# One hybrid decoder layer on one core: 1/rms per token through DRAM, fewer small products, one FFN unit moved

## The chip, the cores and the metric

The kernel runs on one core of a Trainium2 chip. Its engines work at the same time, each through its own queue in order: TensorE (PE in the profile, with its weight loads as PEld), VectorE (DVE), ScalarE (ACT), GpSimd (POOL) and SyncE (SP), which here only issues transfers. POOL issues transfers too. The metric is the device time of one execution in microseconds. The kernel before was run three times: 818.30, 817.38 and 817.83 us, a median of 817.83 us.

## The reference

A decoder layer for 512 tokens of width 1024, in float32. The parts that the change touches:

```python
def rms_norm(x, g):
    xf = x.astype(jnp.float32)
    y = xf * lax.rsqrt(jnp.mean(xf * xf, axis=-1, keepdims=True) + EPS)
    return (y * g.astype(jnp.float32)).astype(x.dtype)

def stick_breaking_attention(q, k, v):
    for i in range(nb):                      # 4 blocks of 128 queries
        z = jnp.einsum('bqhd,bkhd->bhqk', q[:, i * BLOCK:L], k[:, :L]) * (d ** -0.5)
        causal = jnp.arange(L)[None, :] < t
        log_1m = jnp.where(causal, jax.nn.log_sigmoid(-z), 0.0)
        between = lax.cumsum(log_1m, axis=3, reverse=True) - log_1m
        a = jnp.where(causal, jnp.exp(jax.nn.log_sigmoid(z) + between), 0.0)
        outs.append(jnp.einsum('bhqk,bkhd->bqhd', a, v[:, :L]))

def reference(...):
    u = rms_norm(h, ln_mix_pre[l])
    proj = jnp.einsum('bsd,de->bse', u, w_in[l])       # queries, keys, values, gates of three branches
    mkv = jnp.einsum('bmd,de->bme', rms_norm(mem, ln_mem[l]), w_mem_kv[l])
    ...                                                # three attentions, gated, merged, w_out, residual
    a = jax.nn.silu(u @ w_gate[l]) * (u @ w_up[l])     # second norm ahead of it
    ffn = a @ w_down[l]
    h = h + rms_norm(ffn, ln_ffn_post[l])
```

## The kernel before, in words

Each matrix operand is held as two float32r parts, hi and lo: ScalarE rounds to hi (line 134), VectorE subtracts to get lo (line 135), and a product is three matmuls, hi by hi, hi by lo and lo by hi (mm3, lines 166 to 168). Single matmuls go through mm (line 171). On PE the three of an mm3 follow each other; when a weight unit's hi or lo isn't there, PE waits.

Weights come through a Stream. A unit is one block of weights: a load on SP's queue, a split into hi and lo, and the matmuls. Loads run up to four or five units ahead of the matmuls and splits three, in the order in which the units were added. The attention code asks the stream for so many microseconds of matmuls between its own steps, so that PE has work while the other engines do softmax and masks. A planner then orders each engine's instructions: program order is the priority, an instruction is drawn forward when its engine is free and its inputs are there in the planner's estimated times, and code inside tc.high_priority() comes first. Lines 503 to 545 stand in a block whose own order is fixed; other instructions may come between.

Norms. The projections take x times its gain without 1/rms, and the result is scaled as it leaves PSUM. So 1/rms per token is needed in two layouts. rb is a [128 x n] tile with the tokens along the free dimension, the same row in every partition; rs is a [128 x n/128] tile with one token per partition and column. rstd_of (line 218) makes both from the sums of squares per partition: a product with a matrix of ones gives rb's sums in every partition (tile ss_x or ss_m); products of 128 tokens as stationary operand with a single column of ones give rs's (tile st_x for x, a corner of ss_m for mem). Each goes through rsqrt (line 209), two ScalarE and four VectorE instructions. For x, n is 512 and the sums lie in one 512-wide tile. For mem, n is 256 and the tile holds two halves, which the products add in PSUM. rb_x is used by each projection's evacuation (line 288), rs_x by that of the values (L333), rb_m by the memory's keys (line 380), rs_m by its values (line 398).

Values. val (line 322) accumulates 320 columns for four blocks of tokens in four PSUM banks out of a pool of six, first for h = 0, then for h = 1. The banks of the first come free when VectorE has scaled them into v_all (line 333).

Stick-breaking. sb_head (line 605) makes for each of eight heads the scores z of four key blocks in three PSUM tiles, the last two blocks in the same tile, and adds a large negative number on the diagonal blocks by a bf16 product of the identity with the mask, one for each key block (lines 626 and 627).

On POOL lie the casts of constants, the clears of the tiles qbl and kal (line 268), the adds of mem's squares (line 368), the transfers that build the bias (bscr and bias, lines 584 and 593), and later the accumulating loads of the FFN.

FFN. Gate and up are computed for eleven pairs of 128-wide column tiles by a seven-product scheme (p1, p5, p6, p3, p7, p2, p4 for each pair n), each product a unit of 24 matmuls of 256 columns. Its weight operands are sums of weight blocks, made by a plain load on SP (g_raw) and accumulating loads on POOL (g_plus) in a pool of nine buffers, and for p6 and p3 of the later pairs by an add on VectorE as well (g_sum, line 986). The list seq (lines 1230 to 1233) sets the order of the units; the loads are tied to positions in it: for p5 of pair n the plain load four units ahead and the accumulating load two units ahead, and the same for p7. The token operands are called B11, B21, T1, N2, N22, T3 and T4; p3 uses N22, p5 uses T1, p4 uses T4.

Of the kernel before, what the change touches and what calls it, by code (L numbers as in the profile page):

```python
# [10 lines left out]
F32 = mybir.dt.float32  # L11
# [3 lines left out]
ALU = mybir.AluOpType  # L15
AX = mybir.AxisListType

P = 128
D = 1024
S = 512  # L20
# [83 lines left out]
def tile_kernel(ctx, tc, a):  # L104
    nc = tc.nc
# [6 lines left out]
    drm = ctx.enter_context(tc.tile_pool(name="drm", bufs=1, space=bass.MemoryType.DRAM))  # L112
# [3 lines left out]
    cst = first.enter_context(tc.tile_pool(name="cst", bufs=1))  # L116

    def ck(name, dt=F32):
        return ckp.tile([P, 512], dt, tag="ck", name=name)

    def small(name, n=4):
        return sm.tile([P, 8], F32, tag="s", name=name)[:, :n]
# [4 lines left out]
    def aps(name):  # L127
        return psa.tile([P, 512], F32, tag="a", name=name)

    st = {}  # L130
# [33 lines left out]
    def mm3(out, l, r, start, stop):  # L164
        (lh, ll), (rh, rl) = l, r
        nc.tensor.matmul(out, lh, rh, start=start, stop=False, skip_group_check=True)  # L166
        nc.tensor.matmul(out, lh, rl, start=False, stop=False, skip_group_check=True)  # L167
        nc.tensor.matmul(out, ll, rh, start=False, stop=stop, skip_group_check=True)  # L168

    def mm(out, l, r, start, stop):  # L170
        nc.tensor.matmul(out, l, r, start=start, stop=stop, skip_group_check=True)  # L171

    def cols(hl, o, n):
        return hl[0][:, o : o + n], hl[1][:, o : o + n]
# [7 lines left out]
    def fn(*args, **kw):  # L182

        ins = nc.scalar.activation(*args, **kw)  # L184
        for p in pin:
            after(ins, p)
        since.append(ins)
        return ins
# [10 lines left out]
    def const(name, shape, pool=cst):  # L199
        t = pool.tile(shape, F32, name=f"c_{name}")  # L200
        nc.sync.dma_start(t[:, :], a[name])
        return t
# [3 lines left out]
    ones = cst.tile([P, P], F32, name="ones")  # L206
    nc.vector.memset(ones[:, :], 1.0)

    def rsqrt(r, v, t, ss):

        fn(t, ss, AF.Ln, bias=eps_t, scale=1.0 / D)
        nc.vector.tensor_scalar(v, ss, 1.0 / D, EPS, op0=ALU.mult, op1=ALU.add)
        fn(r, t, AF.Exp, scale=-0.5)
        nc.vector.scalar_tensor_tensor(t, r, -0.5, r, op0=ALU.mult, op1=ALU.mult)
        nc.vector.tensor_tensor(t, t, v, op=ALU.mult)
        nc.vector.scalar_tensor_tensor(r, t, 1.5, r, op0=ALU.add, op1=ALU.mult)

    def rstd_of(name, acc, n, bank):


        w = acc.shape[1] // n
        ps = bank(f"ss_{name}")
        for i in range(w):
            mm(ps[:, :n], ones[:, :], acc[:, i * n : (i + 1) * n], i == 0, i == w - 1)
        pt = bank(f"st_{name}")[:, : n // P] if n == S else ps[:, n : n + n // P]
        for t in range(n // P):
            for i in range(w):
                mm(pt[:, t : t + 1], acc[:, i * n + t * P : i * n + (t + 1) * P], ones[:, :1], i == 0, i == w - 1)
        rb = cst.tile([P, n], F32, name=f"rb_{name}")
        v, t = ck(f"v_{name}"), ck(f"t_{name}")  # L230
        rsqrt(rb[:, :], v[:, :n], t[:, :n], ps[:, :n])
        rs = cst.tile([P, n // P], F32, name=f"rs_{name}")
        rsqrt(rs[:, :], small(f"v_{name}", n // P), small(f"t_{name}", n // P), pt)
        return rs, rb

    def gained(x, g, h, l):
# [85 lines left out]
    def val(h, q):  # L322
        def gen(hi, lo):
            if q == 0:
                st["pv"] = [aps(f"pv{h}{t}") for t in range(NT)]
            for i in range(3 if q < 2 else 2):
                k = 3 * q + i
                for t in range(NT):
                    x = (u[k][0][:, t * P : (t + 1) * P], u[k][1][:, t * P : (t + 1) * P])
                    mm3(st["pv"][t][:, :320], x, cols((hi, lo), i * 320, 320), k == 0, k == KC - 1)  # L330
                    yield 0.41
                    if k == KC - 1:
                        nc.vector.tensor_scalar(  # L333
                            v_all[:, t * 640 + h * 320 : t * 640 + (h + 1) * 320],
                            st["pv"][t][:, :320],
                            st["rs"][:, t : t + 1],
                            None,
                            op0=ALU.mult,
                        )

        return gen

    v_all = cst.tile([P, NT * 640], F32, name="v_all")
# [90 lines left out]
    for h in range(2):  # L434
        for q in range(3):
            n = 3 if q < 2 else 2
# [111 lines left out]
    ident = const("ident", [P, P], base)  # L548
    ntri = const("ntri", [P, P])
    nmf = const("negm", [P, P])  # L550
    sinks = cst.tile([P, 8], F32, name="sinks")
    nc.sync.dma_start(sinks[:, :], a["sinks"].to_broadcast([P, 8]))
    identb = cst.tile([P, P], BF16, name="identb")
    nc.gpsimd.tensor_copy(identb[:, :], ident[:, :])
    negm = cst.tile([P, P], BF16, name="negmb")
    nc.gpsimd.tensor_copy(negm[:, :], nmf[:, :])
    ntri_r = cst.tile([P, P], F32R, name="ntri_r")
    nc.gpsimd.tensor_copy(ntri_r[:, :], ntri[:, :])
    none = cst.tile([P, P], F32, name="none")
# [38 lines left out]
    SEG = [(0, 0, 512), (1, 0, 384), (2, 0, 256), (2, 256, 128)]  # L598
# [6 lines left out]
    def sb_head(h):  # L605
        c = h // 2
        ks, qs, ql = (st[(x, c, h % 2)] for x in ("kbs", "qbs", "qbl"))
        z = [aps(f"z{h}{i}") for i in range(3)]

        def seg(ts, j):  # L610
            i, o, n = SEG[j]
            return ts[i][:, o : o + n]

        for j in range(4):
            i, o, n = SEG[j]
            kj = slice(j * P, (j + 1) * P)
            if j < 3:
                out, qh, qlo = z[i][:, o : o + n], qs[:, j * P :], ql[:, j * P :]
            else:

                out = z[i][:, o : o + 2 * n]
                qh = qs[:, j * P :].unsqueeze(1).to_broadcast([P, 2, P])
                qlo = ql[:, j * P :].unsqueeze(1).to_broadcast([P, 2, P])
            mm(out, ks[:, kj], qh, j < 3, False)
            mm(out, ks[:, kj], qlo, False, False)
        for i, o, n in SEG:
            mm(z[i][:, o : o + P], identb[:, :], negm[:, :], False, False)
        e = [ck(f"e{h}{i}") for i in range(3)]
        sh = [ck(f"sh{h}{i}", F32R) for i in range(3)]
        sl = [ck(f"sl{h}{i}", F32R) for i in range(3)]  # L630
        for i in range(3):
            x, n = e[i][:, : W[i]], W[i]
            nc.scalar.activation(x, z[i][:, :n], AF.Abs)
            fn(x, x, AF.Exp, scale=-1.0)
            st["chain"] = fn(x, x, AF.Ln, bias=1.0)
            nc.vector.scalar_tensor_tensor(x, z[i][:, :n], 0.0, x, op0=ALU.max, op1=ALU.add)
            if i == 2:

                nc.vector.tensor_tensor(e[i][:, 384:], e[i][:, 128:256], e[i][:, 256:384], op=ALU.add)
                x, n = e[i][:, :], 512  # L640
            nc.vector.tensor_copy(sh[i][:, :n], x)
            nc.vector.tensor_tensor(sl[i][:, :n], x, sh[i][:, :n].bitcast(F32), op=ALU.subtract)
        yield 7.0

        def both(t):

            return t[2][:, :].rearrange("p (b n) -> p b n", b=4)[:, 0:4:3, :]

        for j in range(3):
            for t in (sh, sl):  # L650
                mm(seg(z, j), ntri_r[:, :], seg(t, j), False, j == 2 and t is sl)
        for t in (sh, sl):
            mm(z[0][:, 128:], none_r[:, :], seg(t, 1), False, False)
        for t in (sh, sl):
# [12 lines left out]
        for j in range(4):  # L667
            for i, x in enumerate((st["even"], e)):
                mm(ys[64 * i : 64 * i + 64, j * P :], vcols(j, 128 + (2 * c + i) * 64), seg(x, j), j == 0, j == 3)
        pair_out(SB, c, ys)  # L670
# [412 lines left out]
    rb = {}  # L1083
    bank = {}
# [143 lines left out]

    fs = Stream(None, f_split, LOAD_AHEAD + 1)
    seq = [("p1", 0), ("p2", 0), ("p1", 1), ("p1", 2), ("p2", 1)]  # L1230
    seq += [("p5", 0), ("p6", 0), ("p3", 0), ("p5", 1), ("p7", 0), ("p6", 1), ("p3", 1), ("p4", 0)]
    for n in range(1, HF):
        seq += [(p, n) for p in PROD if (p, n) not in seq]
    at = {x: i for i, x in enumerate(seq)}
# [166 lines left out]
```

## Time and profile before

| What | Value |
|---|---|
| Median of three runs | 817.83 us |
| Profiled execution, its own time | 818.05 us |
| Its span | 816.3 us |
| PE busy | 806.5 us, 99% |
| VectorE busy | 590.2 us, 72% |
| ScalarE busy | 440.2 us, 54% |
| GpSimd busy | 82.7 us, 10% |
| Granted TensorE clock, mean | 0.999 |
| DMA | 112.93 MB, mean 138 GB/s |

The rows of the timeline read: start in us, duration in us (of the whole run of them, where several are merged), engine, line and operation, tile written and tiles read, form, count, and in brackets how long the engine had been idle and what ended that. A row of waits gives the engine, tile and line that waited, what it waited for, the total in us, how often, and the longest. A window's row gives the length and then, for PE, PEld, DVE, ACT and POOL, the busy time with the number of instructions, then the granted clock, the DMA share and GB/s. A row of a tile or a group gives least, median and greatest duration in ns and the first and last start. A row of DMA issues gives the queue, the count, the size and the median us from issue to landing.

### The profile page before, as it was taken

To read this page: it belongs to the slowest core of one execution; us is meant where nothing else is said; L and a number is where in the kernel's file an instruction comes from. 1 tells how busy PE (TensorE), PEld (TensorE's weight loads), DVE (VectorE), ACT (ScalarE), POOL (GpSimd) and SP (SyncE) were. 2 spreads that over 40 slices of the span, in tenths; PEclk is the share of its full clock that TensorE was granted. 3 is DMA by queue.
4 is the path that set the end of the run, shared out by engine and by line. 5 is a ranking of instruction groups with operands and counts; after the bars stand their busy time and mean duration, and the time that the engine had idled before them with its cause. 6 is when DMAs were issued, how large, how long until landed. Compare 5 with 4: busy or idle time off the path is not lost.

```text
span 816.3 us, 12397 instructions
## 1 busy us (share of the span) xinstructions
PE 806.5 (99%) x4753; PEld 706.6 (87%) x4753; DVE 590.2 (72%) x945; ACT 440.2 (54%) x791; POOL 82.7 (10%) x100
## 2 busy tenths in 40 slices
PE   9999999999999999999999999999999999999996
PEld 6899888778788888888888899999999999988885
DVE  7796768556488853774385869977776767798797
ACT  7453757556555542553362666644444455666573
POOL 3002200000000000231003200010000000205200
PEclk9999999999999999999999999999999999999999
DMA  7434524321221223212359945977777763759902
GB/s 267 141 114 128 190 87 128 85 73 52 78 78 53 78 78 102 79 53 78 103 155 352 254 93 142 247 199 201 183 189 178 185 178 94 169 131 223 213 1 103
DMA packets 37563, 112.93 MB, mean 138 GB/s; under 512 B 4352, under 2 KB 6064, under 8 KB 37504
## 3 DMA queue, kind: packets, MB, share of 16 engines
q1 hardware_dynamic: 29184, 86.32, 33.5%
q0 software_dynamic: 7888, 25.43, 16.4%
q8 instruction: 37, 0.61, 0.3%
q10 hardware_dynamic: 432, 0.39, 0.1%
q14 instruction: 22, 0.18, 0.1%
HBM read 108.46 MB, written 3.67 MB: 137 GB/s over the span
## 4 chain that ended last, share of the span: by engine, by line
PE 94%; DVE 3%; ACT 1%; DMA 1%; issue 0%; ACTq 0%; SPq 0%; DVEq 0%
PE g L166 5%; PE g L167 5%; PE g L168 5%; PE gx L166 5%; PE gx L168 5%; PE gx L167 5%; PE z L171 4%; PE br L166 3%; PE br L167 3%; PE br L168 3%; PE gy L168 3%; PE gy L166 3%; PE gy L167 3%; PE x L167 2%; PE x L166 2%; PE x L168 2%
## 5 line engine op out<-in xcount | busy, mean ns | idle before, releaser
L134 ACT CAST hi<-raw 128x1024 fp32r<-128x1024 f32 (+2 forms) x64 | 65.8, 1034 | 110.1 <-issue 50.2
L134 ACT CAST hi<-gw 128x1024 fp32r<-128x1024 f32 x77 | 79.8, 1048 | 82.2 <-DVE gw L986 40.0
L135 DVE TENSOR_TENSOR lo<-gw,hi 128x1024 fp32r<-128x1024 f32 x77 | 93.5, 1223 | 33.6 <-ACT hi L134 33.6
L135 DVE TENSOR_TENSOR lo<-raw,hi 128x1024 fp32r<-128x1024 f32 (+2 forms) x64 | 78.1, 1220 | 17.6 <-ACT hi L134 17.3
L166 PE MATMUL g<-uh,hi 128*128 128x512 f32 x192 | 75.6, 394 | 0.0
L168 PE MATMUL g<-uh,lo 128*128 128x512 f32 x192 | 74.8, 389 | 0.0
L167 PE MATMUL g<-ul,hi 128*128 128x512 f32 x192 | 74.8, 389 | 0.0
L288 DVE SCALAR_TENSOR_TENSOR g<-g,rb_x 128x512 f32<-128x512 f32 x24 | 16.4, 690 | 55.4 <-PE g L168 55.3
L168 PEld LDWEIGHTS g<-uh,lo 128*128 128x128 f32 x192 | 36.0, 188 | 7.6
L166 PEld LDWEIGHTS g<-uh,hi 128*128 128x128 f32 x192 | 36.1, 188 | 7.5 <-issue 0.3
L968 POOL DMA_DIRECT2D gw<-in_w_gu x27 | 23.4, 905 | 188.8 <-DMA gw<-in_w_gu 81.4
L167 PEld LDWEIGHTS g<-ul,hi 128*128 128x128 f32 x192 | 36.1, 188 | 7.1
L134 ACT CAST hi<-r 128x1024 fp32r<-128x1024 f32 (+1 forms) x24 | 23.6, 982 | 19.9 <-PE y L168 5.3
L167 PE MATMUL x<-lo,lh 128*128 128x512 f32 x88 | 34.2, 389 | 0.0
L166 PE MATMUL x<-hi,lh 128*128 128x512 f32 x88 | 34.2, 389 | 0.0
L168 PE MATMUL x<-hi,ll 128*128 128x512 f32 x88 | 34.1, 389 | 0.0
L135 DVE TENSOR_TENSOR lo<-r,hi 128x1024 fp32r<-128x1024 f32 (+1 forms) x24 | 27.1, 1131 | 3.7 <-ACT hi L134 3.6
L184 ACT ACTIVATE e<-e 128x384 f32<-128x384 f32 (+1 forms) x48 | 26.9, 561 | 1.5
L134 ACT CAST hi<-bp 128x512 fp32r<-128x512 f32 x33 | 19.1, 619 | 13.4 <-PE y L168 4.8
L135 DVE TENSOR_TENSOR lo<-bp,hi 128x512 fp32r<-128x512 f32 x33 | 22.3, 711 | 5.0 <-ACT hi L134 4.9
L166 PE MATMUL gx<-T4h,hi 128*128 128x256 f32 x88 | 25.1, 285 | 0.4 <-ACT hi L134 0.4
L166 PE MATMUL gy<-N22h,hi 128*128 128x256 f32 x88 | 25.1, 285 | 0.2 <-ACT hi L134 0.2
(546 smaller groups left out, 2618.1 us busy)
## 6 DMA issues: line engine op xcount, KB each, us to landing
gw<-in_w_gu SPq DMA_DIRECT2D x57, 512.0 KB, 5.1
raw<-in_w_p SPq DMA_DIRECT2D x38, 512.0 KB, 3.6
gw<-in_w_gu POOLq DMA_DIRECT2D x27, 512.0 KB, 7.9
raw<-in_w_br SPq DMA_DIRECT2D x12, 512.0 KB, 3.8
bp<-in_w_dn SPq DMA_DIRECT2D x22, 256.0 KB, 8.4
r<-in_w_dn POOLq DMA_DIRECT2D x10, 512.0 KB, 8.7
raw<-in_w_out SPq DMA_DIRECT2D x8, 512.0 KB, 3.6
bp<-in_w_dn POOLq DMA_DIRECT2D x11, 256.0 KB, 12.8
```

Of the source, the lines that this page charges most:

```text
L134: ins = nc.scalar.copy(hi, raw)
L135: lows = nc.vector.tensor_tensor(lo, raw, hi.bitcast(F32), op=ALU.subtract)
L166: nc.tensor.matmul(out, lh, rh, start=start, stop=False, skip_group_check=True)
L167: nc.tensor.matmul(out, lh, rl, start=False, stop=False, skip_group_check=True)
L168: nc.tensor.matmul(out, ll, rh, start=False, stop=stop, skip_group_check=True)
L171: nc.tensor.matmul(out, l, r, start=start, stop=stop, skip_group_check=True)
L184: ins = nc.scalar.activation(*args, **kw)
L288: nc.vector.scalar_tensor_tensor(t[:, :], ps[:, :], s, st["rb"][:, :], op0=ALU.mult, op1=ALU.mult)
L968: nc.gpsimd.dma_start(gw[(n, key)][:, :], g_src(n, i, j), accum_op=ALU.add)
```

## The change

Five edits, and a sixth that only moves a load of constants behind two casts in the program.

- rstd_of no longer makes the one-column products and the second rsqrt. For mem, POOL first adds the two halves of the squares, and one product with ones does the sum. When rb is there, its first partition is written to a row in DRAM and read back as the [128 x n/128] tile rs, both by transfers issued on POOL.
- The evacuation of the values stands in tc.high_priority().
- The masks of the last two key blocks, which share a PSUM tile, are added by one product whose output covers both blocks.
- In the FFN's order, p5 of pair 2 (the third) comes ahead of p3 of pair 1.

```diff
     def rstd_of(name, acc, n, bank):
-        w = acc.shape[1] // n
+        if acc.shape[1] > n:
+            nc.gpsimd.tensor_tensor(acc[:, :n], acc[:, :n], acc[:, n : 2 * n], op=ALU.add)
         ps = bank(f"ss_{name}")
-        for i in range(w):
-            mm(ps[:, :n], ones[:, :], acc[:, i * n : (i + 1) * n], i == 0, i == w - 1)
-        pt = bank(f"st_{name}")[:, : n // P] if n == S else ps[:, n : n + n // P]
-        for t in range(n // P):
-            for i in range(w):
-                mm(pt[:, t : t + 1], acc[:, i * n + t * P : i * n + (t + 1) * P], ones[:, :1], i == 0, i == w - 1)
+        mm(ps[:, :n], ones[:, :], acc[:, :n], True, True)
         rb = cst.tile([P, n], F32, name=f"rb_{name}")
         v, t = ck(f"v_{name}"), ck(f"t_{name}")
         rsqrt(rb[:, :], v[:, :n], t[:, :n], ps[:, :n])
+        row = drm.tile([1, n], F32, name=f"row_{name}")
+        nc.gpsimd.dma_start(row[:, :], rb[:1, :])
         rs = cst.tile([P, n // P], F32, name=f"rs_{name}")
-        rsqrt(rs[:, :], small(f"v_{name}", n // P), small(f"t_{name}", n // P), pt)
+        nc.gpsimd.dma_start(rs[:, :], row[:, :].rearrange("o (t p) -> (o p) t", p=P))
         return rs, rb
...
                     if k == KC - 1:
-                        nc.vector.tensor_scalar(
+                        with tc.high_priority():
+                            nc.vector.tensor_scalar(
...
-        for i, o, n in SEG:
-            mm(z[i][:, o : o + P], identb[:, :], negm[:, :], False, False)
+        for i in range(2):
+            mm(z[i][:, :P], identb[:, :], negm[:, :], False, False)
+        blocks23 = z[2][:, :].rearrange("p (b n) -> p b n", b=4)[:, 0:4:2, :]
+        mm(blocks23, identb[:, :], negm[:, :].unsqueeze(1).to_broadcast([P, 2, P]), False, False)
...
-    seq += [("p5", 0), ("p6", 0), ("p3", 0), ("p5", 1), ("p7", 0), ("p6", 1), ("p3", 1), ("p4", 0)]
+    seq += [("p5", 0), ("p6", 0), ("p3", 0), ("p5", 1), ("p7", 0), ("p6", 1), ("p5", 2), ("p3", 1), ("p4", 0)]
```

More of the change, by code (lines that the diff above doesn't have):

```diff
@@ L332, in gen @@
                     if k == KC - 1:
[L333 to L339, printed above, removed]
+                        with tc.high_priority():
+                            nc.vector.tensor_scalar(
+                                v_all[:, t * 640 + h * 320 : t * 640 + (h + 1) * 320],
+                                st["pv"][t][:, :320],
+                                st["rs"][:, t : t + 1],
+                                None,
+                                op0=ALU.mult,
+                            )
         return gen
@@ L550, in tile_kernel @@
     nmf = const("negm", [P, P])
-    sinks = cst.tile([P, 8], F32, name="sinks")
-    nc.sync.dma_start(sinks[:, :], a["sinks"].to_broadcast([P, 8]))
     identb = cst.tile([P, P], BF16, name="identb")
@@ L556, in tile_kernel @@
     nc.gpsimd.tensor_copy(negm[:, :], nmf[:, :])
+    sinks = cst.tile([P, 8], F32, name="sinks")
+    nc.sync.dma_start(sinks[:, :], a["sinks"].to_broadcast([P, 8]))
     ntri_r = cst.tile([P, P], F32R, name="ntri_r")
```

## The prediction

> **What bounds the kernel now.** I read the page first: engine shares, then the chain that ended last.
>
> ```profile
> PE 806.5 (99%) x4753; PEld 706.6 (87%) x4753; DVE 590.2 (72%) x945; ACT 440.2 (54%) x791; POOL 82.7 (10%) x100
> ...
> PE 94%; DVE 3%; ACT 1%; DMA 1%; issue 0%; ACTq 0%; SPq 0%; DVEq 0%
> ```
>
> TensorE (PE) works through 99% of the span and is 94% of the chain. So almost every matmul that goes is time that goes, and a product that starts late is paid in full. Next come the waits of PE alone and the windows in which PE is not full.
>
> ```profile
> PE gx L166 <- ACT hi L134: 0.4, 1, 0.4
> PE pv L166 <- DVE v_all L333: 0.3, 1, 0.3
> ...
> 480.00:520.00 40.00, 39.37 (x326) 38.82 (x324) 37.82 (x66) 28.58 (x56) 2.58 (x3) 1.00 0.51 133
> ```
>
> After the start, where PE waits for its first data, only two places have waits of over 0.2 us: at the value projection (pv, on VectorE's evacuation) and in the FFN's first columns (gx), where the window's third figure shows VectorE (DVE) at 37.82 of 40 us. The diff touches both places. A wait is understated here, because a matmul's drawn duration (0.28 to 0.39 us) is longer than its distance to the next (0.12 to 0.23). I therefore measure by starts, below.
>
> **The change, part by part.**
>
> **1. One-column products of x.** In the PE timeline:
>
> ```profile
> 22.87 1.02 PE L171 MATMUL ss_x<-xacc,ones 128*128 128x512 f32 x2
> 23.73 0.95 PE L171 MATMUL st_x<-ones,xacc 128*128 128x1 f32 x8
> 24.54 0.48 PE L166 MATMUL kb<-uh,hi 128*128 128x512 f32 x1
> ```
>
> The two passes of ss_x take 23.73 - 22.87 = 0.86 us and stay. The eight passes of st_x take 24.54 - 23.73 = 0.81 us and go. The next kb product has its operands, since the wait before it was only its turn. Term: **-0.81 us**. The bounds are 0.7 to 0.81, as its first weight load may lose up to 0.1.
>
> With st_x go two small ScalarE and four small VectorE instructions of about 0.16 us, which overlap; VectorE gains some 0.3 us. The two DRAM transfers wait on POOL for rb_x, which is written at 27.79 + 0.69 = 28.48. Their landing is not in the trace. The nearest rows are POOL's large issues, with medians of 7.9 us (512 KB) and 12.8 us (256 KB) to landing; 2 KB lies below. With nothing as the lower bound and two full 12.8 us in series as the upper, they end between 28.5 and 28.5 + 25.6 = 54.1, while the first reader, the evacuation of v, comes at 66.71:
>
> ```profile
> 27.79 0.69 DVE L216 SCALAR_TENSOR_TENSOR rb_x<-t_x,rb_x 128x512 f32<-128x512 f32 x1
> ...
> gw<-in_w_gu POOLq DMA_DIRECT2D x27, 512.0 KB, 7.9
> ...
> bp<-in_w_dn POOLq DMA_DIRECT2D x11, 256.0 KB, 12.8
> ...
> 15.69 4.45 POOL L268 MEMSET qbl<- 64x512 f32 x8
> 63.03 2.73 POOL L368 TENSOR_TENSOR mT<-mT,mT 128x512 f32<-128x512 f32 x2 [42.89 <-ACT mT L364]
> 66.86 1.28 POOL L368 TENSOR_TENSOR mT<-mT,mT 128x512 f32<-128x512 f32 x1 [1.09 <-ACT mT L364]
> ...
> 66.71 1.92 DVE L333 TENSOR_SCALAR v_all<-pv,rs_x 128x320 f32<-128x320 f32 x4
> ```
>
> So the wait costs nothing. Behind the waiting transfers on POOL come only the adds of mem, at 63.03. Were the qbl clears put behind them too, they would end near 54.1 + 4.5 = 58.6, still ahead of the evacuations of v, which come before the first head. I take 0.
>
> **2. Evacuation of v at high priority.** PE's last product before the wait and the next one:
>
> ```profile
> 66.66 0.31 PE L168 MATMUL pv<-hi,ul 128*128 128x320 f32 x1
> 67.30 0.42 PE L166 MATMUL pv<-hi,uh 128*128 128x320 f32 x1 [0.33 <-DVE v_all L333]
> ...
> L239 DVE SCALAR_TENSOR_TENSOR ml<-mT,xg,mh x8: 479/484/1515, 58.5 to 64.5; 128x256 fp32r<-128x256 f32 x8
> ...
> 65.97 0.81 DVE L135 TENSOR_TENSOR lo<-raw,hi 128x640 fp32r<-128x640 f32 x1
> ```
>
> At its pace of 0.15 us, PE was due at 66.81 and came at 67.30: 0.49 us lost. It waited for the first evacuation (66.71, about 0.5 us: four take 1.92), which stood behind a lo of 0.81 us. Priority lifts the evacuation over that lo. But the last ml starts at 64.5, lasts 1.515 and so ends near 66.0, and VectorE is only some 0.3 us earlier, while PE is now 0.81 earlier. PE wants the bank at 66.81 - 0.81 = 66.0. The evacuation can run from about 65.8 to 66.3. So about 0.3 us of wait stays: term **-0.19 us**. The bounds are -0.49 (no wait) and +0.81 (VectorE not a bit earlier, so that part 1 is eaten here).
>
> **3. Sums of mem.**
>
> ```profile
> 85.33 1.02 PE L171 MATMUL ss_m<-mT,ones 128*128 128x256 f32 x4
> 86.20 0.95 PE L171 MATMUL ss_m<-ones,mT 128*128 128x1 f32 x8
> 87.01 0.48 PE L166 MATMUL ka<-uh,hi 128*128 128x512 f32 x1
> ...
> 90.89 0.69 DVE L642 TENSOR_TENSOR sl<-e,sh 128x512 fp32r<-128x512 f32 x1
> ...
> 93.58 0.28 PE L171 MATMUL z<-sl,ntri_r 128*128 128x256 f32 x1
> ...
> L398 DVE TENSOR_SCALAR mv<-pmv,rs_m x2: 744/744/745, 141.7 to 145.9; 128x512 f32<-128x512 f32 x2
> ```
>
> Four passes take 86.20 - 85.33 = 0.87 us, and two remain: -0.43. The eight one-column passes take 87.01 - 86.20 = 0.81 and go. Term: **-1.25 us**, bounds 1.1 to 1.25. What follows on PE can take it: the second half of head 0 needs sl of its last block, ready at 90.89 + 0.69 = 91.58, and uses it at 93.58, a cover of 2.0 us.
>
> New is a fold on POOL of half the width of the adds above (1.28 us), so about 0.65 us (estimate from those rows; bounds 0.3 and 1.3). It becomes ready at 66.86 + 1.28 = 68.14, and POOL then idles for 14 us; the sum on PE comes at 85.33. It is hidden by 16 us. If that cover is gone, the third rival tells the price. The row and column transfers of mem are first asked for at 141.7 (mv), over 50 us after the sum; two landings of 12.8 us fit twice.
>
> **4. Three mask products for four.**
>
> ```profile
> 82.84 0.28 PE L171 MATMUL z<-qbl,kbs 128*128 128x256 f32 x1
> 82.96 0.40 PE L171 MATMUL z<-negmb,identb 128*128 128x128 bf16 x4
> 83.16 0.48 PE L166 MATMUL ka<-uh,hi 128*128 128x512 f32 x1
> ```
>
> Four products of 128 columns pass in 83.16 - 82.96 = 0.20 us, 0.05 each. The fp32r product ahead of them takes 82.96 - 82.84 = 0.12 for 256 columns, so products go by their columns, and the merged one has 256 of them: 0.10. So 0.05 + 0.05 + 0.10 = 0.20 again: term **0**. Bounds over eight heads: -0.4 (the merged one costs 0.05) to +0.15 (0.12 for it, as the product at 82.84).
>
> The Trainium skill ("TensorE: Matmul & The Clock Gate", section "Back-to-back issue gap") gives about 81 ns for a weight load with a 128-column product and 131 ns with 512. By that, with an estimate of some 100 ns for 256 columns, a head would save about 60 ns and all eight 0.5 us, and the sum would be 3.7. The trace's 50 ns speak against it, so I keep 0.
>
> **5. The unit p5 of the third pair, ahead of p3 of the second.** Here the largest stall sits:
>
> ```profile
> 513.06 0.28 PE L168 MATMUL gx<-N2h,lo 128*128 128x256 f32 x1
> 513.54 0.39 PE L166 MATMUL gy<-N22h,hi 128*128 128x256 f32 x1 [0.19 <-ACT hi L134]
> ...
> 514.48 0.39 PE L166 MATMUL gx<-T4h,hi 128*128 128x256 f32 x1 [0.44 <-ACT hi L134]
> ...
> 515.02 0.28 PE L166 MATMUL gy<-N22h,hi 128*128 128x256 f32 x1
> ...
> 511.12 1.22 DVE L986 TENSOR_TENSOR gw<-gw,gw 128x1024 f32<-128x1024 f32 x1
> ...
> 513.52 2.36 DVE L135 TENSOR_TENSOR lo<-gw,hi 128x1024 fp32r<-128x1024 f32 x2 [0.24 <-ACT hi L134]
> ```
>
> From 513.06 to 515.02 PE started six products; at 0.12 each that is 0.72 of 1.96, so 1.24 us are lost. The unit p3 needs a sum, a hi and a lo (511.12 to 514.7). A whole p5 unit is 24 products of 0.12, 2.88 us, and needs a hi and a lo but no sum. Put between, it moves PE's want of p3 to 516.1. VectorE has one lo of 1.2 us more to do first, so p3's sum ends near 513.5 to 514.4, its hi (1.05) near 514.5 to 515.5 and its lo near 515.7 to 516.7, wanted at 516.3. What is late next is at most some 0.4 us of that lo. Term: **-1.0 us**, bounds -1.24 and 0.
>
> Its data moves too. On SP its raw load takes the place of the raw load of p7, second pair, and POOL's accumulating load follows:
>
> ```profile
> 456.27 0.33 SPq L965 DMA_DIRECT2D gw<-in_w_gu  x1
> 493.91 0.33 SPq L965 DMA_DIRECT2D gw<-in_w_gu  x1
> ...
> 469.21 1.75 POOL L968 DMA_DIRECT2D gw<-in_w_gu  x2 [3.44 <-DMA gw<-in_w_gu]
> 498.09 0.86 POOL L968 DMA_DIRECT2D gw<-in_w_gu  x1 [27.13 <-DVE lo L135]
> ```
>
> By the order in the stream, the loads of p7 sit at 456.27 and in the pair at 469.21, those of p5 at 493.91 and 498.09. They change places: same bytes, same slots. p7's data then lands near 498.1 + 7.9 = 506; its split runs at 514.7 now, so 8 us cover it. The slot that p3's sum frees comes about a unit later, for a load wanted some five units on. I take 0.
>
> **Sum.** 0.81 + 0.19 + 1.25 + 0 + 1.0 = **3.25 us**. The profiled execution took 818.05 us (span 816.3 and 1.75 around it), which gives 814.8. The median of the runs, 817.83, is 0.22 below it, so the predicted time is **814.6 us**. If all bounds fall well, 0.81 + 0.49 + 1.25 + 0.4 + 1.24 = 4.2, so 813.6.
>
> **Rivals.**
>
> (a) **VectorE eats part 1.** From 66 us on, PE is held by the evacuation and not by its own work. If VectorE comes no earlier, 0.81 and 0.19 are lost: 3.25 - 1.0 = 2.25, **815.6**. For it: the ml of 1.515 us against its usual 0.484. Against it: the lo of 0.81 that priority removes. The Trainium skill ("SBUF — State Buffer", section "Who interferes with whom") says that a VectorE instruction with two SBUF inputs and a GpSimd one that reads SBUF lock each other out. The 1515 ns beside the adds on POOL at 63 us agree, and by it no priority shortens this ml.
>
> (b) **The stall of part 5 only moves**, onto p5's split or p3's lo, since VectorE has no room there (37.82 of 40): **815.6**.
>
> (c) **Slower: the fold queues behind the bias loads.** On POOL stand bscr and four loads that wait for its landing:
>
> ```profile
> 82.54 1.07 POOL L584 DMA_DIRECT2D bscr<-brow  x1 [14.18 <-DVE brow L582]
> 89.57 2.89 POOL L593 DMA_DIRECT2D bias<-bscr  x4 [5.96 <-DMA bscr<-brow]
> ```
>
> If the planner puts the fold after them, it ends at 92.46 + 0.65 = 93.1. PE wants it near 85.33 - 1.0 = 84.3 and stands 8.8 us: **823.4**. Behind bscr alone it would end at 84.3, just in time; it decides from the bias loads on. Against it: POOL's ready work has been drawn far ahead (the qbl clears run at 15.69, before rb_x, which their tiles' other halves wait for, is there at 28.48).
>
> (d) **No measurable change.** Another order brings new waits of PE, which has no spare time, and takes back over half: 816.2 to 817.8, say **817.0**. For it: PE's order was planned on estimated times. Against it: outside the two places PE hardly waits.
>
> **How the numbers follow.** Forecast 0.60, (a) 0.10, (b) 0.09, (d) 0.13, (c) and other losses 0.08. Faster means by over 0.2%, 1.6 us, about what a measurement of this kernel can tell from no change: 0.60 + 0.10 + 0.09 = 0.79. Same 0.13, slower 0.08. The range runs from 813.3, the best sum with a little room for the masks, up to 817.2, which takes in (a), (b) and most of (d); (c) is left out.
>
> **What would show it.** Right: kb starts 0.86 us after ss_x, ka 0.43 after ss_m; the four masks' 0.20 us stand; N22 starts within 0.2 us of the last T1 product before it. Wrong: PE waits on POOL before ss_m, a pv wait of over 0.8 us, or waits of PE for hi or lo after 513 us that add up to 1 us.

## The result, and the profile after

The changed kernel takes **813.41 us** (median of six runs, 813.07 to 814.47), the kernel before beside it on the same chip 818.07 us (six runs, 817.38 to 818.96). The ratio is 0.9944, with an interval of 0.9931 to 0.9957: faster by 4.66 us. That was forecast as 3.25 us, so the direction and most of the terms held, and the gain was undersized by 1.4 us. Where those came from is the question of what follows.

The profiled execution took 813.07 us, with a span of 811.3 (before: 818.05 and 816.3). The page of the changed kernel, shares of the engines and of the chain that ended last, and then its waits of PE:

```profile
PE 802.9 (99%) x4727; PEld 704.0 (87%) x4727; DVE 588.7 (73%) x937; ACT 439.6 (54%) x787; POOL 87.5 (11%) x105
...
PE 98%; DMA 0%; ACT 0%; DVE 0%; issue 0%; DVEq 0%
```
```profile
PE warm L171 <- DVE idle L506: 1.3, 1, 1.3
PE kb L167 <- DVE ul L238: 0.3, 1, 0.3
PE gx L166 <- ACT B11h L900: 0.2, 1, 0.2
```

PE does 26 matmuls fewer (of 4753). Its share of the chain went from 94 to 98%, and both waits that were quoted for the kernel before, of pv on v_all and of gx on hi, are gone.

**The two sums.** The PE timeline of the changed kernel, around ss_x and around ss_m:

```profile
22.56 1.02 PE L171 MATMUL ss_x<-xacc,ones 128*128 128x512 f32 x2
23.01 0.80 PE L166 MATMUL kb<-uh,hi 128*128 128x512 f32 x1
23.65 0.40 PE L167 MATMUL kb<-ul,hi 128*128 128x512 f32 x1
...
83.46 0.59 PE L171 MATMUL ss_m<-mT,ones 128*128 128x256 f32 x2
83.70 0.59 PE L166 MATMUL ka<-uh,hi 128*128 128x512 f32 x1
84.12 0.40 PE L167 MATMUL ka<-ul,hi 128*128 128x512 f32 x1
```

The first kb or ka is drawn early and long, at 0.45 and 0.24 after the sum and not at the 0.86 and 0.43 that I had said; its own slow start is in that figure. The second product behind is the safer mark. For x it comes 23.65 - 22.56 = 1.09 us after the sum starts, for mem 84.12 - 83.46 = 0.66. The same marks of the kernel before:

```profile
24.85 0.39 PE L167 MATMUL kb<-ul,hi 128*128 128x512 f32 x1
...
87.33 0.39 PE L167 MATMUL ka<-ul,hi 128*128 128x512 f32 x1
```

They give 24.85 - 22.87 = 1.98 and 87.33 - 85.33 = 2.00. So x gained 0.89 (forecast 0.81) and mem 1.34, or 1.32 by the trace's start times in ns (forecast 1.25).

**The masks.** In the changed kernel, head 0:

```profile
81.14 0.40 PE L171 MATMUL z<-negmb,identb 128*128 128x128 bf16 x3
81.30 0.48 PE L166 MATMUL ka<-uh,hi 128*128 128x512 f32 x1
```

From the first mask to the next start are 0.16 us in place of 0.20. At the resolution of the trace's start times it is 151 ns for 206 in every one of the eight heads, together 0.44 us. The forecast had 0.

**The FFN's second pair.** PE timeline, the changed kernel; T1 is the moved p5, N22 is p3:

```profile
512.19 0.28 PE L168 MATMUL gy<-T1h,lo 128*128 128x256 f32 x1
512.31 0.28 PE L166 MATMUL gy<-N22h,hi 128*128 128x256 f32 x1
512.43 0.28 PE L167 MATMUL gy<-N22l,hi 128*128 128x256 f32 x1
512.55 0.36 PE L166 MATMUL gx<-T4h,hi 128*128 128x256 f32 x1
...
513.22 0.28 PE L166 MATMUL gy<-N22h,hi 128*128 128x256 f32 x1
```

N22 starts 0.12 after the last T1, without a stall. Then the products that use lo come late: from 512.43 to 513.22 PE makes four steps (the rows left out are two starts), which at 0.12 each are 0.48, in 0.79 us. So 0.31 us of the 1.24 are still lost, and 0.93 are gained (forecast 1.0).

**The values.** The waits above hold no wait of pv. In the kernel before, the product behind that wait starts 0.49 us late at 67.30, and the next one is late as well:

```profile
67.56 0.32 PE L167 MATMUL pv<-lo,uh 128*128 128x320 f32 x1
```

To this second start, by which the sums were read too, the wait cost 67.56 - 66.66 - 2 x 0.15 = 0.60. These terms make 0.89 + 1.32 + 0.44 + 0.93 + 0.60 = 4.18. The rest of the 5.0 us between the spans: 0.3 are the first ss_x, which starts earlier (over the kernels below it lies anywhere from 22.2 to 23.0 with the same code ahead of it). 0.2 are lost in the kernel before between heads 0 and 1, where it draws two products of ysb ahead of qa and the changed kernel does not; small_ops below, which draws them ahead too, loses 0.2 in the same place. The last 0.3 lie behind PE's last product. Against the forecast, then, 0.44 come from the masks, 0.15 from the two sums and 0.41 from the wait of pv, which went altogether where I had kept 0.3 of it; the FFN gave 0.07 less, and the start, ysb and the end, 0.8 together, are in none of its terms.

**Why pv no longer waits.** ScalarE's timeline, first before and then after:

```profile
31.55 1.05 ACT L134 CAST hi<-raw 128x1024 fp32r<-128x1024 f32 x1 [3.04 <-DMA raw<-in_w_p]
32.51 1.26 ACT L256 CAST kbs<-kb 64x512 fp32r<-64x512 f32 x2
```
```profile
29.93 1.26 ACT L255 CAST kbs<-kb 64x512 fp32r<-64x512 f32 x2 [2.12 <-DVE kb L287]
31.22 1.05 ACT L134 CAST hi<-raw 128x1024 fp32r<-128x1024 f32 x1
```

Before, ScalarE stood 3.04 us for the load of a weight block, with the casts of kb queued behind it; their input was evacuated by VectorE only at 30.95 + 0.68 = 31.63 (row below, at both_x), just after the load was there. After, kb is evacuated earlier and the planner puts those casts first. VectorE had waited for that hi. Here are these two waits and its last two ml (before), and then the last four ml, the lo behind them and the first evacuations of v (after):

```profile
32.64 1.23 DVE L135 TENSOR_TENSOR lo<-raw,hi 128x1024 fp32r<-128x1024 f32 x1 [1.00 <-ACT hi L134]
...
36.58 1.16 DVE L135 TENSOR_TENSOR lo<-raw,hi 128x960 fp32r<-128x960 f32 x1 [0.59 <-ACT hi L134]
...
63.31 2.74 DVE L239 SCALAR_TENSOR_TENSOR ml<-mT,xg,mh 128x256 fp32r<-128x256 f32 x2 [0.31 <-ACT mh L238]
```
```profile
59.90 2.48 DVE L238 SCALAR_TENSOR_TENSOR ml<-mT,xg,mh 128x256 fp32r<-128x256 f32 x4 [0.30 <-ACT mh L237]
63.70 0.82 DVE L135 TENSOR_TENSOR lo<-raw,hi 128x640 fp32r<-128x640 f32 x1 [1.31 <-ACT hi L134]
64.44 1.92 DVE L333 TENSOR_SCALAR v_all<-pv,rs_x 128x320 f32<-128x320 f32 x4
```

VectorE comes to the evacuation at 64.44 and not at 66.71: 2.27 us earlier, where I had allowed it 0.3, and about 0.9 with the lo that priority was to lift it over. The two waits are 1.59 of it and the small instructions 0.3. A third part is ml: before, two of them were stretched, to 1.30 and 1.52 us, beside POOL's adds of mem's squares; with all work coming earlier only one is, to 1.30, and the last takes 0.47, so the eight together need 1.06 us less. That these parts make more than 2.27 is no contradiction, since VectorE now stands 1.31 us for the hi just ahead of the evacuation. Whether it is this order that decides is asked below.

**POOL**, the changed kernel's timeline, and the landing times of the transfers from the view of DMA:

```profile
28.47 0.68 POOL L230 DMA_DIRECT2D row_x<-rb_x  x1 [13.16 <-DVE rb_x L216]
31.42 0.82 POOL L232 DMA_DIRECT2D rs_x<-row_x  x1 [2.27 <-DMA row_x<-rb_x]
32.28 4.44 POOL L267 MEMSET qbl<- 64x512 f32 x8
...
65.76 0.74 POOL L222 TENSOR_TENSOR mT<-mT 128x256 f32<-128x256 f32 x1
```
```profile
rs_x<-row_x POOLq DMA_DIRECT2D x1, 2.0 KB, 4.2
```

The fold takes 0.74 us (estimated 0.65) and ends 17 us before ss_m needs it. The transfers are done by 31.42 + 4.2, about 35.6, against a first use at 64.44. The clears of qbl did slip behind them, to 32.28, at no cost that the waits of PE show.

### The profile page after: what moved, and what is told of

The parts are those of the page before. It is cut to its first block, busy times and chain, and to the rows that moved or that the text cites. A ratio compares the mean times of both kernels' runs of the same rounds, so it can differ in the third digit from the quotient of the medians.

```text
span 811.3 us, 12342 instructions
## 1 busy us (share of the span) xinstructions
PE 802.9 (99%) x4727; PEld 704.0 (87%) x4727; DVE 588.7 (73%) x937; ACT 439.6 (54%) x787; POOL 87.5 (11%) x105
## 4 chain that ended last, share of the span: by engine, by line
PE 98%; DMA 0%; ACT 0%; DVE 0%; issue 0%; DVEq 0%
PE g L166 5%; PE g L167 5%; PE g L168 5%; PE gx L166 5%; PE gx L168 5%; PE gx L167 5%; PE z L171 4%; PE br L167 3%; PE br L166 3%; PE br L168 3%; PE gy L168 3%; PE gy L166 3%; PE gy L167 3%; PE x L168 2%; PE x L167 2%; PE x L166 2%
## 5 line engine op out<-in xcount | busy, mean ns | idle before, releaser
L166 PE MATMUL gx<-B11h,hi 128*128 128x256 f32 x88 | 25.1, 286 | 0.2 <-ACT B11h L900 0.2
L639 DVE SCALAR_TENSOR_TENSOR e<-z,e 128x384 f32<-128x384 f32 (+1 forms) x24 | 14.3, 598 | 15.0 <-ACT e L184 15.0
```

## The experiments

The changed kernel is the base unless it is said otherwise. All were timed beside the kernel before, whose medians lay between 818.07 and 818.32 us.

**no_dram: the old rstd_of, all else as changed.**

```diff
     def rstd_of(name, acc, n, bank):          # as in the kernel before
-        mm(ps[:, :n], ones[:, :], acc[:, :n], True, True)
+        for i in range(w): mm(ps[:, :n], ones[:, :], acc[:, i * n : (i + 1) * n], i == 0, i == w - 1)
+        ...                                   # one-column products, second rsqrt, no transfers
```

> The changed kernel with rstd_of as it was (one-column products, second rsqrt, mem's halves added in PSUM). My theory: the time of PE's own work comes back, about 0.9 us behind ss_x (second kb product 1.98 us after ss_x starts, as before, against 1.09) and 1.3 us behind ss_m (2.00 against 0.66), and with it VectorE's late evacuation of v, 0.5 us at the value projection, priority or not: 2.5 to 2.8 us in all, near 816.1. Rival: the priority alone removed the wait at the value projection; then it stays away and the kernel is 2.2 us slower, near 815.6.

Measured: 817.39 us (816.38 to 818.01), ratio 0.9989 (0.9979 to 0.9998). So undoing this one part gives back 3.98 of the 4.66 us, while its products are worth 0.89 + 1.32 = 2.21. The PE, ScalarE and VectorE timelines of this kernel:

```profile
66.49 0.31 PE L168 MATMUL pv<-hi,ul 128*128 128x320 f32 x1
67.75 0.42 PE L166 MATMUL pv<-hi,uh 128*128 128x320 f32 x1 [0.94 <-DVE v_all L334]
```
```profile
31.43 1.05 ACT L134 CAST hi<-raw 128x1024 fp32r<-128x1024 f32 x1 [3.08 <-DMA raw<-in_w_p]
```
```profile
66.42 0.81 DVE L135 TENSOR_TENSOR lo<-raw,hi 128x640 fp32r<-128x640 f32 x1
67.16 1.91 DVE L334 TENSOR_SCALAR v_all<-pv,rs_x 128x320 f32<-128x320 f32 x4
```

The wait of pv is back and larger than before, 1.26 - 0.15 = 1.11 us lost (1.2 to the second start), although the evacuation keeps its priority: the lo of 0.81 us that priority was to lift it over still stands ahead of it. The order of ScalarE is the old one as well. With 0.2 for ysb, which is drawn ahead again, and 0.15 for a later ss_x these make 3.8 of the 3.98.

**only_dram: the kernel before with the new rstd_of alone.** Masks, evacuation, order of units and place of the constants are as before.

> The kernel before with the change of rstd_of alone (1/rms through DRAM, the two sums folded first); four mask products, plain evacuation of v, sinks and order of units as before. If the parts are independent and rstd_of is worth the 4.0 us that undoing it cost: 818.2 - 4.0 = 814.2, no wait of pv, second kb 1.1 after ss_x, ka 0.66 after ss_m, a stall of 1.2 at 513. If as forecast for parts 1 and 3 alone: 818.2 - 2.1 = 816.1.

Measured: 814.34 us (814.15 to 814.55), ratio 0.9951 (0.9936 to 0.9966): 3.98 us faster, from the other side. No wait of pv, and the stall of gx and gy on hi (0.4 and 0.2) is still there. That the figure is the same from both sides is in part chance: the wait of pv counts 0.6 here and 1.2 in no_dram, and the first ss_x of this trace starts 0.68 earlier than in the kernel before (22.19 against 22.87). Added up, 3.98 for rstd_of, 0.37 for the masks (mask4, below) and 0.82 for the unit (no_p5) make 5.2 against 4.66 measured; the intervals of the single figures, about 1 us to each side, leave room for that difference.

**no_prio: plain priority for the evacuation of v.**

```diff
-                        with tc.high_priority():
-                            nc.vector.tensor_scalar(...)
+                        nc.vector.tensor_scalar(...)
```

> The changed kernel without high priority for the evacuation of v. If priority removed the wait at the value projection, 0.3 to 0.5 us of it come back (813.8). If it was VectorE's earlier work (my theory now, since its order left waits of 1.0 and 0.6 us for ScalarE before and none after), nothing changes: the step between the last product of h = 0 and the first of h = 1 stays 0.15 us, 813.4.

Measured: 813.27 us (813.22 to 813.62), and no wait of pv. Part 2 of the change is worth nothing that could be measured here; the priority neither removes the wait (no_dram) nor is needed once it is gone.

**pe_ones, small_ops, both_x: which half of the old rstd_of makes the order.** pe_ones keeps the one-column products on PE for x and mem and uses them for nothing. small_ops makes the second rsqrt from columns of ps and uses it for nothing. both_x does both, for x alone. In all three rs still comes through DRAM.

```diff
+        pt = ...                              # pe_ones, both_x: the eight products of one column
+        for t in range(n // P):
+            for i in range(S // n):
+                mm(pt[:, t : t + 1], acc[...], ones[:, :1], i == 0, i == S // n - 1)
         rsqrt(rb[:, :], v[:, :n], t[:, :n], ps[:, :n])
+        un = cst.tile([P, n // P], F32, ...)  # small_ops, both_x: six small instructions
+        rsqrt(un[:, :], small(...), small(...), ps[:, : n // P])   # both_x: from pt
```

> The changed kernel with the one-column products kept on TensorE in both calls of rstd_of (their result is not used; rs still comes through DRAM). Three theories of the 1.7 us beyond the products themselves (the pv wait and the column drawn ahead). (1) Products: the one-column products themselves cause it, by taking TensorE's time or by holding acc longer: second kb 1.98 after ss_x instead of 1.09, second ka 2.0 after ss_m instead of 0.66, and the wait of pv comes back with 0.5 to 1.1: 813.4 + 0.9 + 1.3 + 1.2 = 816.8. (2) Small operations: it is the six small instructions of the second rsqrt that reorder ScalarE and VectorE; with the products alone kept, kbs stays ahead of hi, pv has no wait: 813.4 + 0.9 + 1.0 (for m the late sum does not return) = 815.3.

> The changed kernel with a second rsqrt on [128 x n/128] columns added to both calls of rstd_of (six small instructions on ScalarE and VectorE, result not used); no product is added to TensorE. Theory small operations: ScalarE takes hi (waiting some 3 us for its load) ahead of the kbs casts again, VectorE is 2 us later, the v_all evacuation comes later and pv waits 0.5 to 1.1 on v_all: 813.4 + 0.8 = 814.2 to 814.7; second kb stays 1.09 after ss_x. Theory products: nothing changes, 813.4, no wait of pv.

> The changed kernel with the eight one-column products and the second small rsqrt put back for x alone (result not used; rs_x still comes through DRAM), m as changed. Either of the two alone left pv without a wait. Theory order of ScalarE: both together bring back the order in which ScalarE waits about 3 us for the load of hi ahead of the kbs casts; VectorE then stands about 1.0 and 0.6 for it, mT comes about 2 to 5 later, pv waits 0.5 to 1.1 on v_all and ysb is drawn ahead again (0.2): 813.4 + 0.9 + 0.7 to 1.3 = 815.0 to 815.6. Theory that the way of rs decides (it is late or early by the way it comes, not by the order): no wait of pv, 813.4 + 0.9 = 814.3.

Measured: pe_ones 815.19 us (814.78 to 816.24), small_ops 813.66 us (813.34 to 813.95), both_x 814.97 us (814.48 to 815.87). pe_ones costs 1.78, twice 0.89, so that is the price of eight one-column passes; nothing else came back, so the theory that the products cause the wait fell. small_ops added no wait of pv either, so the theory of the small operations fell too, in the form that they do it alone. With both together, the ScalarE and the PE timeline of both_x:

```profile
30.95 1.05 ACT L134 CAST hi<-raw 128x1024 fp32r<-128x1024 f32 x1 [2.94 <-DMA raw<-in_w_p]
```
```profile
66.15 0.31 PE L168 MATMUL pv<-hi,ul 128*128 128x320 f32 x1
67.26 0.41 PE L166 MATMUL pv<-hi,uh 128*128 128x320 f32 x1 [0.80 <-DVE v_all L341]
```

The old order stands, ScalarE waits 2.94 us, and pv loses 1.11 - 0.15 = 0.96 us. The way of rs is the same as in the changed kernel, so it does not decide. Order and wait go together in all fourteen traces: the kernel before, no_dram and both_x have the old order and a wait of pv, the other eleven the new order and none. No run sets ScalarE's order by itself, and a later evacuation of kb goes with it (next), so which of the two brings the wait is not shown. One part of the expectation missed: ysb, which the kernel before draws ahead of qa, is not drawn ahead in both_x, but is in small_ops, so it does not follow this order.

What goes with the order is when VectorE evacuates kb, which those casts read: at 30.95 and not at 29.21 (before and then after).

```profile
30.95 0.68 DVE L288 SCALAR_TENSOR_TENSOR kb<-kb,rb_x 128x512 f32<-128x512 f32 x1
```
```profile
29.21 0.68 DVE L287 SCALAR_TENSOR_TENSOR kb<-kb,rb_x 128x512 f32<-128x512 f32 x1
```

rb_x is not what separates them, since it starts 4.92 us after ss_x in both. But in the kernel before VectorE takes two lo and the four small instructions between rb_x and this evacuation, in the changed kernel one lo. Counted from the start of ss_x the evacuation comes after 8.08 us in each of the three kernels with the old order, after 7.07 in small_ops and after 6.65 in the other ten. That the planner expected the weight block between 7.07 and 8.08 is argued from the orders, not shown: its estimates are in no trace.

**no_p5: the old order of the units.**

```diff
-("p6", 1), ("p5", 2), ("p3", 1), ("p4", 0)]
+("p6", 1), ("p3", 1), ("p4", 0)]
```

> The changed kernel with the old order of the FFN's units. Theory: the stall of 1.24 us between the last N2 product of pair 1 and the sixth start behind it comes back whole, against 0.3 us left in the changed kernel: 0.9 us slower, near 814.3. Rival: with the rest of the change PE comes 3.7 us earlier and VectorE too, and the stall has changed by itself; then the difference is under 0.4 us.

Measured: 814.23 us (813.93 to 814.45), 0.82 more. The waits of its PE show the old stall again, in the same size as in the kernel before:

```profile
PE gx L166 <- ACT hi L134: 0.4, 1, 0.4
```

**mask4, mask8, mask_first, mask_wide: what a mask product costs.** Four products of 128 columns; eight of 64; the three with the merged one first; the merged one with 512 columns, two blocks of them zeros.

```diff
-        for i in range(2): mm(z[i][:, :P], identb, negm, ...)      # 128 and 128
-        mm(blocks23, identb, negm twice, ...)                      # 256
+        for i, o, n in SEG: mm(z[i][:, o : o + P], identb, negm)   # mask4: 128 x 4
+        for i, o, n in SEG: for q in (0, 64): mm(...64 columns)    # mask8: 64 x 8
+        mm(blocks23, ...); for i in range(2): mm(...)              # mask_first: 256, 128, 128
+        ...; mm(z[2][:, :], identb, negm4)                         # mask_wide: 128, 128, 512
```

> The changed kernel with four mask products a head. Theory by count: each product with its weight load takes PE about 0.05 us whatever its width up to 256, so from the first mask to the second product behind the masks 0.52 us instead of 0.46, eight times 0.05: 0.4 us slower, near 813.8. Theory by columns (the prediction): no change, 813.4.

> The changed kernel with the mask added in eight products of 64 columns a head, in place of three of 128, 128 and 256: the same 512 columns, the same sums. Theory columns: as with four products, 813.4 to 813.8. Theory count of products (about 0.05 us for each load and product, however narrow): five more a head x 8 heads x 0.05 = +2.0, 815.4.

> The changed kernel with the merged mask product of 256 columns issued first and the two of 128 columns behind it (the same three products, the same sums). Starts in the runs so far: 67, 56, 28 ns with three, 67, 56, 56, 28 with four, 39, seven of 29, 29 with eight of 64 columns. So a product costs by its columns (56 for 128, 29 for 64), and the last of a group always 28, whatever its width: theory the last is hidden behind the slow start of the 4-byte product that follows. Then here 67 + 48 (another 128 columns) + 56 + 28, first mask to the next start 0.20 again in place of 0.15, +0.05 x 8 heads = +0.4: 813.8. Theory that the repeated 256 columns, read twice from the same 128, cost as 128, or that products count: 0.15, 813.4.

> The changed kernel with the merged, last mask product 512 columns wide in place of 256 (zeros in the two other blocks, the same sums). Theory hidden last product: its 512 columns are about 0.22 by 56 ns for 128; the slow start behind it covers about 0.11 (28 to the next start and 316 to the second, against 231 between such products: 344 - 231), so the second product behind comes about 0.10 later, 0.57 after the first mask in place of 0.47: +0.8 over eight heads, 814.2. Theory count: 0.47 still, 813.4.

Measured: mask4 813.78 us, mask8 814.04 us, mask_first 813.70 us, mask_wide 814.04 us, that is 0.37, 0.63, 0.29 and 0.63 above the changed kernel. The intervals of these times are some 1.3 us to each side, so the totals alone decide little; the start times do. PE timeline of head 0 in mask_wide:

```profile
81.33 0.38 PE L171 MATMUL z<-negm,identb 128*128 128x512 bf16 x1
81.36 0.58 PE L166 MATMUL ka<-uh,hi 128*128 128x512 f32 x1
81.78 0.40 PE L167 MATMUL ka<-ul,hi 128*128 128x512 f32 x1
```

The same for all five from the trace's start times, in ns from each start to the next, head 0; behind the bar the step from the next product (ka) to the second:

```
mask4       128 128 128 128     67  55  56  28                  | 316
changed     128 128 256         67  56  28                      | 316
mask_first  256 128 128        120  56  28                      | 316
mask_wide   128 128 512         67  56  28                      | 420
mask8       eight of 64         39  29  29  29  29  30  29  29  | 314
```

Two theories fell here. After mask4 I held that products cost by their count, about 0.05 us each; mask8 was to show +2.0 us by that and showed 243 - 151 = 92 ns a head. Products go by their columns, 56 ns for 128 and 29 for 64 (and the first of a group 11 more). The Trainium skill ("TensorE: Matmul & The Clock Gate", section "Wait — 56ns, not 53.3ns?") gives the columns at 2.4 GHz and about 2.5 ns, 56 for 128 columns, and the trace agrees with 55 to 57. The 81 ns for a pair with its weight load that the Trainium skill gives (the same page, section "Back-to-back issue gap"), which I had weighed in the forecast, occur in none of these groups, though each of their products has its weight load. But the last product of the group is followed after 28 ns whatever its width, 64, 128 or 256, and the next step is 316 in each case. So the last one is covered by the slow start of the 4-byte product behind it. How much is covered shows in mask_wide: its next step is 104 longer, so of the 218 ns that 512 columns would take (29 for 64, and 27 for each 64 more) some 114 were hidden. Put the other way, from the start of the last mask product to the second start behind it are 344 ns for up to 256 columns and 448 for 512; less the 231 between 4-byte products in a row, a last product takes 113 ns up to 256 columns and 217 for 512. The merged 256 columns, 110 ns, just fit in that. And mask_first, where the wide one isn't last, is back at 204 with three products, as the theory of the hidden last product said.

**fold_late: the third rival made real.** The fold is ordered behind the last load of the bias on POOL.

```diff
-            nc.gpsimd.tensor_tensor(acc[:, :n], acc[:, :n], acc[:, n : 2 * n], op=ALU.add)
+            fold = nc.gpsimd.tensor_tensor(acc[:, :n], acc[:, :n], acc[:, n : 2 * n], op=ALU.add)
+            after(fold, st["bias_dma"])
```

> The changed kernel with the fold of the memory sums ordered behind the last load of the bias on GpSimd, as the third rival of the forecast had it. If TensorE's stream stands in order at ss_m until then: the bias loads end about 90, the fold takes 0.74, ss_m starts about 91 in place of 83.5, 7 to 9 lost: 820.5 to 822.5, with a wait of PE for GpSimd of that size. If the planner draws other products ahead of ss_m, most of it is hidden: 813.4 to 815.

Measured: 817.64 us (815.82 to 818.05), 4.2 more than the changed kernel, and below either of the rival's figures (8.8 in the forecast, 7 to 9 here). Its POOL and PE timelines:

```profile
90.46 0.73 POOL L222 TENSOR_TENSOR mT<-mT 128x256 f32<-128x256 f32 x1
```
```profile
91.25 0.70 PE L171 MATMUL ss_m<-mT,ones 128*128 128x256 f32 x2 [2.65 <-POOL mT L222]
91.60 0.74 PE L171 MATMUL z<-sh,ntri_r 128*128 128x512 f32 x1
...
95.34 0.48 PE L166 MATMUL qa<-uh,hi 128*128 128x512 f32 x1
```

The fold came as late as the rival had it (90.46), but the planner drew the rest of ka and the next head's z ahead of ss_m, and PE stood only 2.65 us. The remaining 1.6 us are lost behind the wait: from the first z with sh to qa PE needs 95.34 - 91.60 = 3.74 us, and 90.87 - 88.77 = 2.10 in the changed kernel, whose rows these are:

```profile
88.77 0.48 PE L171 MATMUL z<-sh,ntri_r 128*128 128x512 f32 x1
...
90.87 0.47 PE L166 MATMUL qa<-uh,hi 128*128 128x512 f32 x1
```

The windows of fold_late show why. Their last but two figure is the granted clock:

```profile
92.00:93.00 1.00, 1.00 (x4) 0.81 (x4) 0.45 (x2) 0.88 (x2) 0.35 (x1) 0.50 0.85 328
...
94.00:95.00 1.00, 1.00 (x7) 1.00 (x6) 0.78 (x2) 0.00 (x0) 0.00 (x0) 0.50 0.39 156
95.00:96.00 1.00, 1.00 (x7) 0.91 (x7) 0.00 (x0) 0.85 (x2) 0.00 (x0) 0.87 0.20 70
```

After the wait of 2.65 us TensorE ran at half its clock for about 3.4 us, and 2.65 + 1.64 = 4.3 is the whole difference. This is one profiled execution, of 817.56 us. Of the eight, five took 817.56 to 818.05 us with a mean granted clock of 0.995 or 0.996, and three 815.82 to 816.41 with 0.997 or 0.998: 1.7 us less, the size of the loss by the clock. So the half clock probably stayed away in these three and the wait alone cost them some 2.6; only the one execution was profiled, so this is not shown.

## Why the prediction was right, and where it was not

**Part 1** (0.81) was right in kind and a little small: 0.89. pe_ones gives the same 0.89 for eight one-column passes. Both lie past the bound of 0.81. My worry that the next product's first weight load would lose some of it pointed the wrong way.

**Part 2** (0.19) failed at the step "VectorE is only some 0.3 us earlier, while PE is now 0.81 earlier", and with it at "about 0.3 us of wait stays". VectorE came 2.27 us earlier. I had counted the small instructions that go and not asked what the planner would do with ScalarE's queue, where the wait of 3.04 us for a load stood ahead of the casts of kb. I had also taken the ml of 1.515 us as fixed, and it is gone. "Priority lifts the evacuation over that lo" failed too: in no_dram the lo stands ahead of the evacuation all the same. no_dram and both_x show that with the old order the wait is there, although both have the priority; no_prio shows that with the new order no priority is needed. The place gained 0.49 to the first start, which was my lower bound, and 0.60 to the second, and through rstd_of, not through the edit to which I had put the gain.

**Part 3** (1.25) held: 1.32, which is 0.43 for the two passes of 215 ns that went and 0.89 for the eight one-column passes, as for x. The fold is 0.74 us and hidden, as said.

**Part 4** (0) failed at the step "so 0.05 + 0.05 + 0.10 = 0.20 again". That products go by their columns was right, but I read the sum only up to the next start and took each product as paid. The last of the group is hidden behind the product that follows; merging moved one block of 128 columns into that cover. It gave 0.44, just past the bound of -0.4. That the 0.5 us in the forecast's other sum lies near this is chance: its price of a pair is not what these groups show.

**Part 5** (1.0) held: 0.93 by the starts, 0.82 by no_p5. What was late next was the lo of p3, for 0.31 us, as the forecast had it ("at most some 0.4 us of that lo").

**The rivals.** (a), VectorE eating part 1, went the other way: the wait disappeared, and with it the long ml that spoke for this rival. (b), a stall that only moves, is refused by the waits of PE, which hold none for hi or lo behind 513 us. (c) did not happen, and fold_late shows that its price of 8.8 was twice what it would have cost, 4.2 in the median, since the planner does not leave PE standing in program order. (d), no measurable change, is excluded by the interval.

The time lies near the lower end of the range, 813.3, since the pv wait came out at its favourable bound and the masks and both sums a little past theirs. The gain of 4.66 is more than the 4.2 of all favourable bounds together; that the time is still inside, by 0.1 us, is owed to the room left below 813.6, and so in part to luck.

## What to carry to other kernels

Where an engine's row shows a long wait for a load with other work queued behind it, a small saving ahead of it can flip the planner's order, and what that is worth is not read from the instructions saved: here 2.2 us of products brought 4.0, of it 0.6 to 1.2 by a wait of PE 35 us later. The cost of a small product has to be measured to the second start behind its group, because the last of a group can be hidden by the product that follows; merge so that the widest one is last. A price for "the engine stands" needs two corrections, what the planner draws ahead of the wait and what the clock does after it.

## What the runs showed of the hardware that I had not expected

- After a wait of PE of 2.65 us the granted clock stood at 0.50 from about 92 to 95.3 us; 1.6 us of the loss came after the wait was over. By their times, three of the eight executions went without this. The Trainium skill ("TensorE: Matmul & The Clock Gate", section "What's actually happening") has the half clock after an idle window of about 3.4 us and a like time to come back; the way back agrees, while the idle time that sufficed here was shorter.
- Behind a group of bf16 products, a 4-byte product of 512 columns hides about 114 ns of the last of them: it starts 28 ns after it and has 316 ns to its second start, against 231 between such products in a row.
- A round trip of 2 KB through DRAM, issued on POOL, took from 28.47 to about 35.6 us, 7 us for two transfers, 4.2 us of it the landing of the one that scatters a row over partitions.
